# A hybrid decoder layer on one core: mask tiles in another pool, a reordered last head, two spare tiles in the output projection, later E loads, five buffers for the modulation sums

## The chip, the cores and the metric

The kernel runs on one core of a Trainium2 chip. TensorE (PE) multiplies matrices, VectorE (DVE) and ScalarE (ACT) do elementwise work, GpSimd (POOL) some masks, and SyncE (SP), ACT and POOL issue DMAs. Each engine takes its instructions in order, from a queue of its own, and waits on semaphores for the others. The metric is the device time of one execution in microseconds; the median of several runs counts.

## The reference

One layer, sequence 1024, width 1024, float32. The parts that matter here:

```python
mod = c_act @ w_ada + b_ada                # shifts, scales, gates: six vectors of 1024
u = x * (1.0 + sc1) + sh1
proj = u @ w_in                            # qa, ka, va, dq, dk, dv, z, b, a, g_a, g_b
y_a = sliding_window_attention(qa, ka, va, sinks) @ w_oa
# gated DeltaNet, 8 heads of 128, chunks of 64: decay matrices E, a triangular solve, a scan
o = gated_delta_rule(q, k, v, beta, g)
o = o * rsqrt(mean(o * o) + RMS_EPS) * norm_w * silu(z)
y_b = o @ w_ob
mixed = (sigmoid(g_a) * y_a + sigmoid(g_b) * y_b) @ w_out
x = layer_norm(ALPHA * x + (1.0 + gt1) * mixed)
# then the squared-ReLU MLP with 4096 hidden columns, and the second layer norm
```

## The kernel before

Every float32 product of the large projections is made of three: an operand is split into a high and a low part (`uh`, `ul` of the activations, `wh`, `wl` of the weights), and PE adds `uh*wh`, `ul*wh` and `uh*wl`. ACT copies the high part, DVE subtracts it from the raw tile to give the low one (for streamed weights the line with `wl<-wr,wh`). A *unit* (`stream_unit`) is one block of 128 output columns: two halves of 8 x 3 matmuls 128x512.

The program goes through these stages. First come the modulation, the value and key projections, and for each of the 8 DeltaNet heads the function `decays`: it makes `re` and `e` (the decay matrix E), `kd`, the products `kk` of a head's keys (`a<-kT`) and `mt`, and stores them in DRAM (`re_d`, `e_d`, `kd_d`, `md_d`, `l21_d`, which the trace calls `l_d`). In this stage the order of the engines comes from a scheduler; the tiles lie in the pool `pa`. From position `Q0` on the order is the program's own: `at(p, f)` puts the work of `f` at PE matmul number `p` (count[0]), `after(n, f)` at n later, and `vec`, `act`, `now` do so with a planner (`window`) that looks for room on DVE or ACT between the links of the scan. There `pa` is closed and the pool `pb` opens in its memory, with the tiles of the attention. The units of the remaining projections are PE's stream; the attention, the triangular solve (on DVE) and the scan over the heads are put between them.

In the scan head h starts at `R = R0 + 120 h` (PER = 120). `hd_load` fetches kT, E, Re, kd; `hd_kq` uses E (line 1189); `hd_a`, `hd_b`, `hd_c` make the chain over the eight chunks (`rhs`, `vn`, `o`, `St`); `hd_norm` with its `root` takes a square root on ACT, followed by a dummy SiLU that brings the SiLU table back; `hd_silu` is SiLU of z, `hd_out` multiplies and stores `og_d`. At the same time the modulation vectors that are needed later are summed up on DVE: `ada_load` fetches 128x512 of `w_ada` every 14 positions, `ada_add` adds it up (`ada<-adaw`). Units of kind `g_b` end in `gb_done`: copy on ACT (`gz`), store from ACT's queue.

At `OA` the output projection of the attention begins: products `(i, m)` of 12 matmuls each over operands `wo` and `q` (line 1558), in the order (0,1), (1,1), (0,6), (1,6), (0,7), (1,7), (0,4), (1,4), ... ; `q_part` splits the last pieces of the attention's result (`ts` into `qh`, `ql`, "11", "T2", "T3", "T4"). Each product is evicted by `o_part` (line 1510) into a tile of `o_tile`: tag `t0` in the pool `yo`, or `t` in the pool `p2`. `p2` exists only from position `CLOSE` on (`open_p2`), which closes the scan's pools and issues the first loads of further operands (`or`).

Of the kernel before, what the change touches and what calls it, by code (L numbers as in the profile page):

```python
# [9 lines left out]
F32 = mybir.dt.float32  # L10
F32R = mybir.dt.float32r
BF16 = mybir.dt.bfloat16
AF = mybir.ActivationFunctionType
ALU = mybir.AluOpType
# [3 lines left out]
P = 128  # L18
# [4 lines left out]
HALF = 512  # L23
# [4 lines left out]
NEG = -1e30  # L28
# [6 lines left out]
def hybrid_layer_kernel(ctx: ExitStack, tc: tile.TileContext,  # L35
                        x, c, w_ada, b_ada, w_in, conv_w, a_log, dt_bias, sinks, dn_norm_w,
                        w_oa, w_ob, w_out, ln1_g, ln1_b, w_ff1, b_ff1, w_ff2, b_ff2,
                        ln2_g, ln2_b, out, dbg=None):
    nc = tc.nc
    x, c, out = x[0], c[0], out[0]  # L40
# [6 lines left out]
    V, A, G, T = nc.vector, nc.scalar, nc.gpsimd, nc.tensor  # L47
# [9 lines left out]
    def brief(shape, name):  # L57
        return gpool.tile(shape, F32, name=name, bufs=1)
# [7 lines left out]
    def bc(ap, shape):  # L66
# [7 lines left out]
    gb_d = dram.tile([KT, P, S], F32, name="gb_d")  # L74
    og_d = dram.tile([KT, P, S], F32, name="og_d")
    kt_d = dram.tile([8, P, S], F32, name="kt_d")
    kd_d = dram.tile([8, P, S], F32, name="kd_d")
    e_d = dram.tile([8, P, S], F32, name="e_d")
# [17 lines left out]
    make_identity(nc, ident)  # L96
    ones = const.tile([P, P], F32, name="ones")
    V.memset(ones, 1.0)
    tri = brief([P, P], "tri")
    G.affine_select(out=tri, in_=ones, pattern=[[1, P]], compare_op=ALU.is_ge, fill=0.0,  # L100
                    base=0, channel_multiplier=-1)
    trim = brief([P, P], "trim")
    amask = brief([P, 2 * P], "amask")
    V.memset(amask, 0.0)
    G.affine_select(out=amask[:, 0:P], in_=amask[:, 0:P], pattern=[[1, P]], compare_op=ALU.is_gt,
                    fill=NEG, base=0, channel_multiplier=-1)
    G.affine_select(out=amask[:, P:2 * P], in_=amask[:, P:2 * P], pattern=[[-1, P]],
                    compare_op=ALU.is_ge, fill=NEG, base=0, channel_multiplier=1)
    eps_ln = const.tile([P, 1], F32, name="eps_ln")
    V.memset(eps_ln, LN_EPS)  # L110
    eps_rms = const.tile([P, 1], F32, name="eps_rms")
# [84 lines left out]
    halves = [slice(0, HALF), slice(HALF, 2 * HALF)]  # L196


    events, count, order = [], [0], [0]

    def at(p, f, *args):
        order[0] += 1
        heapq.heappush(events, (p, order[0], f, args))

    def after(n, f, *args):
        at(count[0] + n, f, *args)
# [86 lines left out]
    pv_pool = tc.tile_pool(name="pv", bufs=1, side="right")  # L293
    pv = pv_pool.__enter__()
    NV = 272
    wvh = pv.tile([P, KT, NV], F32R, name="wvh")
    wvl = pv.tile([P, KT, NV], F32R, name="wvl")
    p0_pool = tc.tile_pool(name="p0", bufs=1, side="right")
# [162 lines left out]
    for step in steps.split():  # L461
        f, k = step[0], int(step[1])
# [49 lines left out]
    with tc.tile_pool(name="pa", bufs=2, side="right") as pa:  # L512
        if True:
            ba = pv.tile([P, NT, 16], F32, name="ba")
            for t in range(NT):
                tok = slice(t * P, (t + 1) * P)
                pt = psum("ab"[t % 2], 2) if t < 4 else mm_tile()
# [29 lines left out]
            xs, y, r, z2, pl = (tmp(n) for n in ("xs", "y", "r", "z2", "pl"))  # L547
# [85 lines left out]
        for h in range(8):  # L633
# [41 lines left out]
            for b in range(2):  # L675
                r = slice(64 * b, 64 * b + 64)
# [15 lines left out]
    pb = pb_pool.__enter__()  # L692
    M = so.tile([P, 64, 64], F32, name="M")
    Mf = M.rearrange("p s c -> p (s c)")

    def solve_load():
        nc.scalar.dma_start(out=Mf, in_=md_d.rearrange("h b n s c -> (h b n) (s c)"))

# [258 lines left out]
    def big4(tag, dtype=F32, shape=None, bufs=2):  # L957
        return pc.tile(shape or [P, S], dtype, tag=tag, name=tag, bufs=bufs)

    HOP = 5  # L960
    PER = 3 * HOP * NT
    R0 = Q0 + 160
# [17 lines left out]
    def vec(lag, cost, f, *args):  # L980
        q = window("V", count[0] + lag, cost)
        at(q, f, *args)
        return q
# [64 lines left out]
    def ada_cols_of(f):  # L1048
        return (2, 5, 3, 4)[f // 2] * D + (f % 2) * HALF

    def ada_load(i, f, k):
        w, lo = ada["w"][i % 3], ada_cols_of(f)
        nc.sync.dma_start(out=w, in_=w_ada[k * P:(k + 1) * P, lo:lo + HALF])
        q = vec(36, 3.3, ada_add, w, k)
        if k == KT - 1:
            at(q + 7, ada_part, f)

# [42 lines left out]
    def hd_load(h):  # L1100
        d = heads[h]
        d["kT"], d["kd"], d["E"], d["Re"] = big4("kT"), big4("kd"), big4("E"), big4("Re", bufs=1)
        TT = d["TT"] = TTs[h % 2]
        T2o = d["T2o"] = big4("T2o", shape=[64, 4, 64], bufs=1)
        half = [slice(0, 64), slice(64, P)]
        nc.sync.dma_start(out=d["kT"], in_=kt_d[h])
        (nc.sync if h else nc.gpsimd).dma_start(out=d["E"], in_=e_d[h])
        nc.gpsimd.dma_start(out=T2o, in_=tt_d[h, 1, 1::2].rearrange("n s c -> s n c"))
        for i in range(2):
            nc.gpsimd.dma_start(out=TT[half[i], :, half[i]], in_=tt_d[h, i].rearrange("n s c -> s n c"))  # L1110
        nc.gpsimd.dma_start(out=d["Re"], in_=re_d[h])
        nc.gpsimd.dma_start(out=d["kd"], in_=kd_d[h])
        if h == 0:
            hd_solved(0)
        elif h < 7:
            hd_solved(h + 1)
        d["ssq"] = pc.tile([P, NT], F32, tag="ssq", name="ssq")
        d["sso"] = pc.tile([P, NT], F32, tag="sso", name="sso")
        d["vr"] = big4("vr")
        d["o"] = [big4(f"o{i}", shape=[P, HALF], bufs=2 - i) for i in range(2)]  # L1120
# [142 lines left out]
    def hd_norm(h):  # L1263
        d = heads[h]
        fs = pc.tile([P, NT], F32, tag="fs", name="fs")
        V.tensor_scalar(out=fs, in0=d["ssq"], scalar1=RMS_EPS * P * P, scalar2=None, op0=ALU.mult)
        V.tensor_tensor(out=fs, in0=fs, in1=d["sso"], op=ALU.add)

        def sc(n):
            if n % 2:  # L1270
                A.activation(out=o_chunk(d, n), in_=o_chunk(d, n), func=AF.Copy, scale=fs[:, n:n + 1])
            else:
                V.tensor_scalar(out=o_chunk(d, n), in0=o_chunk(d, n), scalar1=fs[:, n:n + 1], scalar2=None,
                                op0=ALU.mult)
        def root():
            A.activation(out=fs, in_=fs, func=AF.Sqrt, scale=1.0 / P, bias=eps_q)
            A.activation(out=d["sso"][:, 0:1], in_=d["ssq"][:, 0:1], func=AF.Silu)
            vec(9, 0.5, lambda: V.reciprocal(out=fs, in_=fs))
            vec(11, 5.5, lambda: [sc(n) for n in range(0, NT, 2)])
            act(11, 7, lambda: [sc(n) for n in range(1, NT, 2)] + [flags.add(("o", h))])  # L1280
        act(3, 13.5, root)

    def hd_out(h, half):
        d = heads[h]
        assert ("o", h) in flags
        tp = psum("b", 2)
        for j in range(4):
            T.transpose(tp[:, chunk(j)], o_chunk(d, 4 * half + j), ident)

        def put():  # L1290
            V.scalar_tensor_tensor(out=d["sz"][:, halves[half]], in0=tp, scalar=normw, in1=d["sz"][:, halves[half]],
                                   op0=ALU.mult, op1=ALU.mult)
            if half == 1:
                nc.gpsimd.dma_start(out=og_d[h], in_=d["sz"])
        now("V", 2, 3.3, put)

    def gb_done(i):
        ts = []

        def done(half, pt):  # L1300
            t = big4("gz", shape=[P, HALF])
            A.activation(out=t, in_=pt, func=AF.Copy)
            A.dma_start(out=gb_d[i, :, halves[half]], in_=t)
        return done

    for h in range(8):
        R = R0 + PER * h
        early = max(R - 118, OPEN + 1)
        at(early, hd_load, h)
        for half in range(2):  # L1310
            at(R - 45 + 15 * half, hd_kq, h, half)
            at(R - 40 + 15 * half, hd_qturn, h, half)
            at(R - 10 + 15 * half, hd_vturn, h, half)
            at(R + 122 + 8 * half, hd_silu, h, half)
        if h == 0:
            at(early + 50, hd_z, 0)
            at(early + 52, hd_solved, 1)
        at(R - 55 if h else R0 - 30, hd_x, h)
        at(R + 35, hd_gate, h)
        for n in range(NT):  # L1320
            at(R + 3 * HOP * n, hd_a, h, n)
            at(R + 3 * HOP * n + HOP, hd_b, h, n)
            at(R + 3 * HOP * n + 2 * HOP, hd_c, h, n)
        at(R + PER + 2, hd_norm, h)
        at(R + PER + (45 if h < 7 else 32), hd_out, h, 0)
        at(R + PER + (60 if h < 7 else 36), hd_out, h, 1)

    big2 = p2 = p2_pool = None
    L0 = Q0 + 48 * (len(units_h) - 1)
# [51 lines left out]
        split_s(*[t[:, k % 2, :] for t in quad[name, k // 2]], late[k][i][:, halves[u]], 5)  # L1381

    for name, ps_ in (("11", (-42, -39, -36, -33)), ("T2", (-29, -26, -23, -20)), ("T3", (-9, -6, 0, 4)),
                      ("T4", (8, 11, 16, 19))):
        for k in range(4):
            at(OA + ps_[k], q_part, name, k)

# [56 lines left out]
            stream_unit(uh, ul, gb_done(h), interleave=h == 7)  # L1444


    CLOSE = OA + 22
    oh, ol, ograw = [None] * KT, [None] * KT, {}

    def og_load(k):  # L1450
# [46 lines left out]
    ot = {}  # L1497

    def o_tile(i, c):
        if (i, c) in ((0, 0), (0, 2), (2, 0), (2, 2)):  # L1500
            ot[i, c] = yo.tile([P, HALF], F32, tag="t0", name="t0")
        else:
            ot[i, c] = p2.tile([P, HALF], F32, tag="t", name="t", bufs=5)
        return ot[i, c]
# [357 lines left out]
    def put(m, i, t, q=None):  # L1862
        (q or nc.sync).dma_start(out=hf_d[m - 1, i], in_=t)
# [428 lines left out]
```

## Time and profile before

| | |
|---|---|
| median of 3 runs | 1809.24 us (1808.39 to 1811.13) |
| the profiled execution | 1811.05 us, its span 1809.3 us |
| granted TensorE clock, mean | 0.995 |
| DVE, ACT, POOL busy | 72%, 58%, 18% |
| DMA, mean over the span | 194 GB/s |

The span runs from the first to the last instruction. A line of a timeline gives the start and the length of a group of instructions in us, the engine, the line in the kernel, the operation, output<-inputs with shapes, and in brackets the idle time just before it with what ended it. PE rows show the time until a result is out, about 0.39 us for a 128x512 matmul; as they are pipelined, the step from one to the next counts.

### The profile page before, as it was taken

The page shows a single profiled execution, that of the slowest core. Times are in us where ns is not written, and L with a number is a line of the kernel's source. Part 1 is how long each engine was busy: PE and PEld are TensorE (multiplying, and loading weights), DVE is VectorE, ACT ScalarE, POOL GpSimd, SP SyncE. Part 2 cuts the span into 40 slices and gives each one's busy share as a digit, 9 for nine tenths or more (in the row PEclk, how much of TensorE's full clock was granted, in tenths as well). Part 3 has the DMA queues.
Part 4 walks back from the last instruction along what each step waited for, and adds up shares of the span by engine and source line. Part 5 has one row for each costly group of instructions (what it writes and reads, how often), then busy time and mean ns, then how long its engine had stood idle before and what let it go on. Part 6 is the DMA issues. An engine that isn't in the chain of part 4 may idle for free.

```text
span 1809.3 us, 26356 instructions
## 1 busy us (share of the span) xinstructions
PE 1787.6 (99%) x9137; PEld 1504.0 (83%) x9137; DVE 1300.7 (72%) x2438; ACT 1046.4 (58%) x2371; POOL 318.8 (18%) x482
## 2 busy tenths in 40 slices
PE   8999999999999999999999999999999999999998
PEld 6988888888888888888878888878888888888887
DVE  6688688988856566767678455789777766676697
ACT  4699678888874556556475332475555554434341
POOL 0234234444331011110001210002222220000000
PEclk8999999999999999999999999999999999999999
DMA  9756722232256566655747644459887879755671
GB/s 280 207 201 204 229 71 90 62 110 74 85 195 199 137 178 177 171 182 176 245 141 249 215 151 143 147 163 333 284 287 272 287 275 391 250 187 186 204 262 47
DMA packets 268151, 350.32 MB, mean 194 GB/s; under 512 B 27009, under 2 KB 172114, under 8 KB 267762
## 3 DMA queue, kind: packets, MB, share of 16 engines
q1 hardware_dynamic: 225842, 220.27, 38.9%
q0 software_dynamic: 31728, 107.39, 17.7%
q10 hardware_dynamic: 10448, 20.98, 3.2%
q8 instruction: 72, 1.18, 0.3%
q14 instruction: 61, 0.50, 0.1%
HBM read 238.74 MB, written 107.75 MB: 191 GB/s over the span
## 4 chain that ended last, share of the span: by engine, by line
PE 89%; ACT 3%; DVE 2%; DMA 2%; issue 1%; POOL 0%; ACTq 0%; DVEq 0%; POOLq 0%
PE mm L262 34%; PE mm L2153 8%; PE mm L2213 7%; PE a L2213 4%; PE b L2153 4%; PE b L2213 4%; PE a L2153 3%; PE mm L1558 2%; PE mm L1782 2%; PE c L2213 2%; PE c L892 2%; PE a L1782 1%; PE b L1558 1%; PE mm L192 1%; PE mm L190 1%; PE mm L191 1%
## 5 line engine op out<-in xcount | busy, mean ns | idle before, releaser
L262 PE MATMUL mm<-uh,wh 128*128 128x512 f32 x800 | 319.8, 400 | 0.0
L262 PE MATMUL mm<-uh,wl 128*128 128x512 f32 x800 | 319.6, 399 | 0.0
L262 PE MATMUL mm<-ul,wh 128*128 128x512 f32 x800 | 318.8, 398 | 0.0
L220 DVE TENSOR_TENSOR sp<-sraw,sp 128x1024 fp32r<-128x1024 f32 x112 | 132.7, 1219 | 75.8 <-ACT sp L219 75.8
L219 ACT ACTIVATE sp<-sraw 128x1024 fp32r<-128x1024 f32 x112 | 112.6, 1053 | 121.4 <-PE b L2213 75.4
L262 PEld LDWEIGHTS mm<-uh,wh 128*128 128x128 f32 x800 | 150.7, 188 | 26.4
L262 PEld LDWEIGHTS mm<-ul,wh 128*128 128x128 f32 x800 | 150.8, 188 | 26.1
L262 PEld LDWEIGHTS mm<-uh,wl 128*128 128x128 f32 x800 | 150.8, 188 | 26.0
L2213 PE MATMUL mm<-sp 128*128 128x512 f32 x528 | 136.0, 389 | 0.0
L2213 PEld LDWEIGHTS mm<-sp 128*128 128x128 f32 x528 | 98.7, 188 | 20.5 <-DVE sp L220 0.2
L2213 PE MATMUL a<-sp 128*128 128x512 f32 x336 | 92.2, 389 | 0.0
L825 DVE CUSTOM_DVE_ANT_0 nscore<-a,amask,nsink 128x256 f32<-128x256 f32 (+1 forms) x128 | 54.5, 464 | 43.4 <-PE a L818 43.1
L1236 ACT ACTIVATE vn<-a,brk 128x128 f32<-128x128 f32 x64 | 23.6, 368 | 98.0 <-PE a L1234 95.9
L2213 PE MATMUL b<-sp 128*128 128x512 f32 (+1 forms) x336 | 79.6, 374 | 0.0
L2213 PEld LDWEIGHTS a<-sp 128*128 128x128 f32 x336 | 63.1, 188 | 13.1
L237 DVE TENSOR_TENSOR wl<-wr,wh 128x1024 fp32r<-128x1024 f32 x56 | 69.0, 1232 | 3.5 <-ACT wh L233 3.4
L836 POOL TENSOR_TENSOR sm<-sm 128x256 f32<-128x256 f32 x56 | 51.5, 920 | 103.6 <-ACT sm L832 72.8
L2213 PEld LDWEIGHTS b<-sp 128*128 128x128 f32 x336 | 60.3, 188 | 11.2
L220 DVE TENSOR_TENSOR wl<-fraw,wh 128x1024 fp32r<-128x1024 f32 x43 | 52.5, 1222 | 19.7 <-ACT wh L219 19.5
L832 ACT ACTIVATE sm<-nscore,stat 128x257 f32<-128x257 f32 (+1 forms) x128 | 62.0, 487 | 2.7 <-DVE stat L825 2.5
L219 ACT ACTIVATE wh<-fraw 128x1024 fp32r<-128x1024 f32 x43 | 45.0, 1055 | 31.0 <-PE b L2153 25.1
L877 POOL TENSOR_SCALAR_AFFINE_SELECT pl<-ph 128x512 fp32r<-128x512 f32 x56 | 53.7, 959 | 41.7 <-DVE ph L870 38.1
(563 smaller groups left out, 4757.6 us busy)
## 6 DMA issues: line engine op xcount, KB each, us to landing
wr<-in_w_in_dram SPq DMA_DIRECT2D x60, 512.0 KB, 3.8
sraw<-hf_d SPq DMA_DIRECT2D x54, 512.0 KB, 4.3
adaw<-in_w_ada_dram SPq DMA_DIRECT2D x74, 256.0 KB, 5.0
fraw<-in_w_ff_dram SPq DMA_DIRECT2D x32, 512.0 KB, 5.1
sraw<-wt_d SPq DMA_DIRECT2D x32, 512.0 KB, 4.3
hf_d<-t ACTq DMA_DIRECT2D x48, 256.0 KB, 4.5
wt_d<-wx POOLq DMA_DIRECT2D x48, 256.0 KB, 3.9
sraw<-in_w_ff_dram SPq DMA_DIRECT2D x22, 512.0 KB, 5.8
```

Of the source, the lines that this page charges most:

```text
L219: A.activation(out=hi, in_=src, func=AF.Copy)
L220: after(lag, lambda: V.tensor_tensor(out=lo, in0=src, in1=hi.bitcast(F32), op=ALU.subtract))
L237: V.tensor_tensor(out=hl[1], in0=raw, in1=hl[0].bitcast(F32), op=ALU.subtract)
L262: T.matmul(ts[half], lhsT=w[:, k, :], rhs=xx[k][:, sl], start=k == 0 and m == 0, stop=k == KT - 1 and m == 2)
L825: V.tensor_tensor_reduce(out=ns[:, i, 1:1 + W], in0=sc[:, i * 2 * P:i * 2 * P + W], in1=amask[:, mo:mo + W], scale=-1.0, scalar=nsink[:, 2 ...
L832: A.activation(out=sm[:, i, 0:1 + W], in_=ns[:, i, 0:1 + W], func=AF.Exp, scale=-1.0, bias=st[:, i:i + 1], accum_out=st[:, 2 + i:3 + i])
L836: G.tensor_tensor(out=sm[:, :, 1 + P:1 + 2 * P], in0=sm[:, :, 1:1 + P], in1=sm[:, :, 1 + P:1 + 2 * P], op=ALU.add)
L877: G.affine_select(out=flat4(part), in_=flat4(full), pattern=[[0, 4], [1 if odd else -1, P]], compare_op=ALU.is_ge if odd else ALU.is_gt, f ...
L1558: T.matmul(pt, lhsT=t[:, lw, k, :], rhs=r[:, k % 2, :], start=begin and k == 0 and x_ == 0, stop=k == 3 and x_ == 2, skip_group_check=True)
L1782: T.matmul(pt, lhsT=m[k][:, tok], rhs=w[:, k % 2, :], start=k == 0 and w is wh and m is mh, stop=k == KT - 1 and m is ml)
L2153: T.matmul(pt, lhsT=a[:, kk, :], rhs=b[k], start=begin and k == 0 and x_ == 0, stop=k == 3 and x_ == 2, skip_group_check=True)
L2213: T.matmul(to, lhsT=a[:, f, t * P:(t + 1) * P], rhs=b[:, f, lo:up], start=(begin or own) and s % NS == 0 and f == 0 and x_ == 0, stop=s % ...
```

## The change

It has six parts.

1. The masks `tri` and `trim` move from the start to the pool `pv`; `amask`, the mask of the attention, moves from the start of the program to the opening of `pb`.
2. The sums of the modulation get two more buffers (tiles with tag `t0`), five instead of three, and an add is due 42 instead of 36 positions after its load.
3. E of the heads 1 to 7 is loaded 40 positions later.
4. In the last head the SiLU of z stands 22 to 25 positions earlier, ahead of the root, and the dummy SiLU is left out; the output's halves come 3 positions earlier, and each is stored by itself on SP instead of one store on POOL.
5. `gb_done` places copy and store a little later where they would fall close ahead of `vn`.
6. The tiles of the products with c = 0 all use `t0`, with two buffers; `T4` is split 8 to 11 positions later and `p2` opens 10 positions later.

```diff
-    tri = brief([P, P], "tri")
-    ...
-    amask = brief([P, 2 * P], "amask")
-    V.memset(amask, 0.0)
     ...
+    tri = pv.tile([P, P], F32, name="tri")
     ...
     pb = pb_pool.__enter__()
     ...
+    amask = pb.tile([P, 2 * P], F32, name="amask", bufs=1)
+    V.memset(amask, 0.0)
+    G.affine_select(out=amask[:, 0:P], ...)
+    G.affine_select(out=amask[:, P:2 * P], ...)
     ...
     def ada_load(i, f, k):
-        w, lo = ada["w"][i % 3], ada_cols_of(f)
+        if i == 0:
+            ada["w"] += [yo.tile([P, HALF], F32, tag="t0", name="adaw", bufs=2) for _ in range(2)]
+        w, lo = ada["w"][i % 5], ada_cols_of(f)
         nc.sync.dma_start(out=w, in_=w_ada[k * P:(k + 1) * P, lo:lo + HALF])
-        q = vec(36, 3.3, ada_add, w, k)
+        q = vec(42, 3.3, ada_add, w, k)
     ...
-        (nc.sync if h else nc.gpsimd).dma_start(out=d["E"], in_=e_d[h])
+        if h:
+            after(40, lambda: nc.sync.dma_start(out=d["E"], in_=e_d[h]))
+        else:
+            nc.gpsimd.dma_start(out=d["E"], in_=e_d[h])
     ...
         def root():
             A.activation(out=fs, in_=fs, func=AF.Sqrt, scale=1.0 / P, bias=eps_q)
-            A.activation(out=d["sso"][:, 0:1], in_=d["ssq"][:, 0:1], func=AF.Silu)
+            if h < 7:
+                A.activation(out=d["sso"][:, 0:1], in_=d["ssq"][:, 0:1], func=AF.Silu)
     ...
-            if half == 1:
+            if h == 7:
+                nc.sync.dma_start(out=og_d[h, :, halves[half]], in_=d["sz"][:, halves[half]])
+            elif half == 1:
                 nc.gpsimd.dma_start(out=og_d[h], in_=d["sz"])
     ...
         def done(half, pt):
-            t = big4("gz", shape=[P, HALF])
-            ...
+            def put():
+                ...
+            p = count[0]
+            r = (p - R0) % 15
+            at(p + 7 - r if 2 < r < 7 else p, put)
     ...
-            at(R + 122 + 8 * half, hd_silu, h, half)
+            at(R + (122 + 8 * half if h < 7 else 100 + 5 * half), hd_silu, h, half)
     ...
-        at(R + PER + (45 if h < 7 else 32), hd_out, h, 0)
-        at(R + PER + (60 if h < 7 else 36), hd_out, h, 1)
+        at(R + PER + (45 if h < 7 else 29), hd_out, h, 0)
+        at(R + PER + (60 if h < 7 else 33), hd_out, h, 1)
     ...
-                      ("T4", (8, 11, 16, 19))):
+                      ("T4", (16, 19, 27, 30))):
     ...
-    CLOSE = OA + 22
+    CLOSE = OA + 32
     ...
     def o_tile(i, c):
-        if (i, c) in ((0, 0), (0, 2), (2, 0), (2, 2)):
-            ot[i, c] = yo.tile([P, HALF], F32, tag="t0", name="t0")
+        if c == 0:
+            ot[i, c] = yo.tile([P, HALF], F32, tag="t0", name="t0", bufs=2)
```

How it moves instructions shows at three places; all lines of the changed kernel up to the masks' new place have numbers lower by 6 to 10, those behind it higher by up to 13. The first is the end of `decays` on DVE. Before, at the beginning of head 6's second part (`rk` to `kd` belong to the head, `wl` is the low part of weights of a unit after `Q0`):

```order
L604 TENSOR_SCALAR e<-a,r 128x128 x4
L652 RECIPROCAL rk<-irk 128x8
L237 TENSOR_TENSOR wl<-wr,wh 128x1024
L653 TENSOR_TENSOR brk<-beta,rk 128x8
L656 TENSOR_TENSOR kdc<-ekd,rk 128x8
L654 SCALAR_TENSOR_TENSOR nbrk_684<-brk,rk 128x8
```

After, the end of the same stage, head 7 (`kll` and `qs` are the attention's keys and queries):

```order
L648 SCALAR_TENSOR_TENSOR nbrk_676<-brk,rk 128x8
L654 TENSOR_TENSOR kd<-b,kdc 128x512
L654 TENSOR_TENSOR kd<-c,kdc 128x512
L666 SCALAR_TENSOR_TENSOR mt<-a,nbrk_676,e 128x128 x8
L691 MEMSET amask 128x256
L227 TENSOR_TENSOR wl<-wr,wh 128x1024 x2
L767 TENSOR_TENSOR kll<-ks,khh 64x512 x3
L227 TENSOR_TENSOR wl<-wr,wh 128x1024
L767 TENSOR_TENSOR kll<-ks,khh 64x512
L787 SCALAR_TENSOR_TENSOR qs<-mm,qs 64x512 x4
```

The memset of `amask` now stands behind the last `mt` of head 7, and the `wl` of the first two units, one of which stood between `rk` and `brk` of head 6 (the other one head earlier), stand behind the memset.

The second place is PE there. Before, from the first matmul of the first unit (`uh_127` and `ul_135` are block 0 of the activations, `a<-kT` the `kk` of head 7):

```order
L262 MATMUL mm<-uh_127,wh 128x512
L262 MATMUL mm<-ul_135,wh 128x512
L262 MATMUL mm<-uh_127,wl 128x512
L262 MATMUL mm<-uh_128,wh 128x512
L262 MATMUL mm<-ul_136,wh 128x512
L669 MATMUL a<-kT 128x128 x4
L262 MATMUL mm<-uh_128,wl 128x512
L262 MATMUL mm<-uh_129,wh 128x512
L262 MATMUL mm<-ul_137,wh 128x512
L262 MATMUL mm<-uh_129,wl 128x512
L262 MATMUL mm<-uh_130,wh 128x512
L669 MATMUL a<-kT 128x128 x4
```

After (block 0 is `uh_116` and `ul_124`):

```order
L252 MATMUL mm<-uh_123,wl 128x512
L252 MATMUL mm<-uh_116,wh 128x512
L252 MATMUL mm<-ul_124,wh 128x512
L663 MATMUL a<-kT 128x128 x4
L252 MATMUL mm<-uh_116,wl 128x512
L252 MATMUL mm<-uh_117,wh 128x512
L252 MATMUL mm<-ul_125,wh 128x512
L252 MATMUL mm<-uh_117,wl 128x512
```

The first matmul on `wl` stood ahead of both `kk` groups; now it stands behind them, as the unit's third matmul.

The third place is ACT at the beginning of the output projection, before:

```order
L1302 ACTIVATE gz<-mm 128x512
L1303 DMA gb_d<-gz 128x512
L219 ACTIVATE wo<-owg 128x512
L219 ACTIVATE qh<-ts 128x512 x2
L219 ACTIVATE wo<-owr 128x512
L219 ACTIVATE qh<-ts 128x512
L1510 ACTIVATE t_10286<-mm 128x512
L219 ACTIVATE qh<-ts 128x512
L219 ACTIVATE wo<-owg 128x512
L219 ACTIVATE wo<-owr 128x512
L219 ACTIVATE qh<-ts 128x512
L1510 ACTIVATE t<-mm 128x512
```

After:

```order
L1312 ACTIVATE gz<-mm 128x512
L1313 DMA gb_d<-gz 128x512
L1312 ACTIVATE gz<-mm 128x512
L1313 DMA gb_d<-gz 128x512
L209 ACTIVATE wo<-owr 128x512
L1523 ACTIVATE t_10283<-mm 128x512
L209 ACTIVATE qh<-ts 128x512
L209 ACTIVATE wo<-owg 128x512
L209 ACTIVATE wo<-owr 128x512
L209 ACTIVATE qh<-ts 128x512
L1523 ACTIVATE t_10310<-mm 128x512
```

`t` are the evictions of the first two products, `qh` on `ts` the split pieces, `wo` on `owr` and `owg` the operands. Between the root and the first `t` stood nine splits `qh`, three `wo`, one SiLU of z and a second table load (`L1277 ACT_TABLE_LOAD`); now seven `qh` and three `wo`, without SiLU and table load.

More of the change, by code (lines that the diff above doesn't have):

```diff
@@ L98, in hybrid_layer_kernel @@
     V.memset(ones, 1.0)
-    tri = brief([P, P], "tri")
-    G.affine_select(out=tri, in_=ones, pattern=[[1, P]], compare_op=ALU.is_ge, fill=0.0,
-                    base=0, channel_multiplier=-1)
-    trim = brief([P, P], "trim")
-    amask = brief([P, 2 * P], "amask")
-    V.memset(amask, 0.0)
[L105 to L108, printed above, removed]
     eps_ln = const.tile([P, 1], F32, name="eps_ln")
@@ L295, in hybrid_layer_kernel @@
     NV = 272
+    tri = pv.tile([P, P], F32, name="tri")
+    G.affine_select(out=tri, in_=ones, pattern=[[1, P]], compare_op=ALU.is_ge, fill=0.0,
+                    base=0, channel_multiplier=-1)
+    trim = pv.tile([P, P], F32, name="trim")
     wvh = pv.tile([P, KT, NV], F32R, name="wvh")
@@ L694, in hybrid_layer_kernel @@
     Mf = M.rearrange("p s c -> p (s c)")
+    amask = pb.tile([P, 2 * P], F32, name="amask", bufs=1)
+    V.memset(amask, 0.0)
+    G.affine_select(out=amask[:, 0:P], in_=amask[:, 0:P], pattern=[[1, P]], compare_op=ALU.is_gt,
+                    fill=NEG, base=0, channel_multiplier=-1)
+    G.affine_select(out=amask[:, P:2 * P], in_=amask[:, P:2 * P], pattern=[[-1, P]],
+                    compare_op=ALU.is_ge, fill=NEG, base=0, channel_multiplier=1)
     def solve_load():
@@ L1300, in done @@
         def done(half, pt):
-            t = big4("gz", shape=[P, HALF])
-            A.activation(out=t, in_=pt, func=AF.Copy)
-            A.dma_start(out=gb_d[i, :, halves[half]], in_=t)
+            def put():
+                t = big4("gz", shape=[P, HALF])
+                A.activation(out=t, in_=pt, func=AF.Copy)
+                A.dma_start(out=gb_d[i, :, halves[half]], in_=t)
+            p = count[0]
+            r = (p - R0) % 15
+            at(p + 7 - r if 2 < r < 7 else p, put)
         return done
```

## The prediction

> **What bounds the kernel now.** I read the page first: the engines' busy time, the slices with the granted TensorE clock, and the chain that ended last.
>
> ```profile
> span 1809.3 us, 26356 instructions
> ## 1 busy us (share of the span) xinstructions
> PE 1787.6 (99%) x9137; PEld 1504.0 (83%) x9137; DVE 1300.7 (72%) x2438; ACT 1046.4 (58%) x2371; POOL 318.8 (18%) x482
> ...
> PE 89%; ACT 3%; DVE 2%; DMA 2%; issue 1%; POOL 0%; ACTq 0%; DVEq 0%; POOLq 0%
> ```
>
> PE is busy 99% of the span and is 89% of the chain, so the time moves only by what makes PE stand still, or by its clock. Next I took the table of what PE waited for (total, times, longest), since every row of it is a gain that the change could have.
>
> ```profile
> PE mm L1558 <- ACT t L1510: 2.9, 2, 1.5
> ...
> PE c L1257 <- DVE o L1261: 0.9, 1, 0.9
> ...
> PE b L1288 <- DVE o L1273: 0.7, 1, 0.7
> PE a L1245 <- ACT vn L1236: 0.6, 1, 0.6
> ```
>
> The first row is the output projection, the next three are the scan over the heads. All four together are 5.1 us, 0.3% of the time: that is nearly all this change can win. From three runs within 0.15%, no change means about 0.2%, or 3.6 us. What is left to find is what it can lose, and that needs the places where instructions now stand elsewhere.
>
> **The masks.** `amask` now lives in the pool `pb`, which opens on the memory of the closed pool `pa`. Its memset therefore waits for the last readers of `pa`: head 7's `mt`, and the stores of `kd`, `md`, `l` (SP) and `re`, `e` (POOL) out of it. As one reader is a store, the wait ends only when it has landed. Behind that memset in DVE's queue stand the two `wl` subtractions for the first two units of the next stage; before, they stood in heads 5 and 6 of `decays`. The timelines of DVE, SP, ACT and PE at that place (start, length, what):
>
> ```profile
> 202.38 2.16 DVE L672 SCALAR_TENSOR_TENSOR mt<-a,nbrk,e 128x128 f32<-128x128 f32 x8 [1.27 <-POOL e L608]
> 209.85 2.00 DVE L766 TENSOR_TENSOR kll<-ks,khh 64x512 fp32r<-64x512 f32 x3 [5.31 <-ACT khh L761]
> 212.11 1.23 DVE L237 TENSOR_TENSOR wl<-wr,wh 128x1024 fp32r<-128x1024 f32 x1 [0.26 <-ACT wh L233]
> ...
> 205.99 0.65 SPq L678 DMA_DIRECT2D l_d<-mt  x1
> ...
> 209.19 0.63 ACT L761 ACTIVATE khh<-ks 64x512 fp32r<-64x512 f32 x1 [8.00 <-DMA l_d<-mt]
> ...
> 201.16 1.05 PE L669 MATMUL a<-kT 128*128 128x128 f32 x8
> 201.97 0.48 PE L262 MATMUL mm<-ul,wh 128*128 128x512 f32 x1
> ...
> 221.26 0.11 DVE L700 MEMSET M<- 128x64 f32 x1
> ...
> 202.21 17.69 PE mm L262 x78
> ```
>
> The row at 209.19 shows the mechanism in the old kernel: `khh`, also a tile of `pb`, held ACT 8.00 us until `l_d` had landed. It cost nothing, as PE needed none of it. The new memset is the same wait, but on DVE, with work behind it that PE needs.
>
> When would PE get there? The last row gives the dense step, 17.69 / 78 = 0.227 us. At 201.97 the old PE had done both `kk` groups of head 7 and ten matmuls of the first unit; in the new order the third matmul of that unit (the first on `wl`) comes after both groups and two, so PE is there at 201.97 - 8 x 0.227 = 200.15. When is `wl` ready? In the old kernel the stores had landed by 209.19. Two `wl` of 1.23 have left DVE ahead of head 7's chain, but that chain also runs through ACT and POOL (`mt` waited 1.27 for POOL), so I take 1.0 us earlier, between 0 and 2.46. The memset is 128x256; 128x64 took 0.11, so between 0.11 and 0.44, I take 0.25 as nearer to a fixed part plus four times the work. Then 208.2 + 0.25 + 1.23 = 209.7, and PE stands from 200.15 to 209.7: +9.5 us (8.0 to 10.7). Nothing covers it: the instruction behind it on PE is the same unit, in order. ACT and DVE run late by no more than PE does, so nothing is late next. Of the rest of this part, `tri` in another pool and POOL's two selects (POOL is busy 18%) cost nothing: the scores that use the masks come behind the same stall.
>
> The Trainium skill, DMA: Bandwidth & Descriptors, Anatomy of one DMA, puts a DMA's fixed cost at some 2 us, mostly the receipt of the last byte. By it the 64 KB store issued at 205.99 would be in at about 208.0 and the stall 1.2 us shorter, by an estimate from that figure; the 3.2 us from issue to `khh` in the row decide.
>
> **The clock after such a pause.** The windows of 1 us around the start (PE busy is the second number, PEclk the first after the engines):
>
> ```profile
> 31.00:32.00 1.00, 0.06 (x1) 0.00 (x0) 0.65 (x2) 0.00 (x0) 0.00 (x0) 1.00 1.14 310
> 32.00:33.00 1.00, 0.41 (x3) 0.33 (x3) 0.96 (x5) 0.59 (x1) 0.00 (x0) 1.00 0.91 256
> 33.00:34.00 1.00, 1.00 (x5) 0.84 (x6) 0.82 (x3) 1.00 (x3) 0.00 (x0) 0.84 1.03 292
> 34.00:35.00 1.00, 1.00 (x4) 0.81 (x3) 0.98 (x2) 1.00 (x2) 0.00 (x0) 0.50 1.06 289
> ...
> 37.00:38.00 1.00, 1.00 (x12) 1.00 (x10) 0.22 (x1) 0.00 (x0) 0.00 (x0) 0.95 1.14 317
> ...
> 931.00:935.00 4.00, 2.72 (x12) 2.17 (x12) 4.00 (x8) 3.32 (x7) 0.00 (x0) 1.00 0.33 133
> ```
>
> After 1.5 us without work (31 to 33) the clock was 0.50 from about 33.7 to 37.1: 0.32 us of the first slice, three whole ones, 0.1 of the last, 3.4 us. In the projection 1.3 us of idle time in four did not lower it. A pause of 9.5 us is six times the one that did, so I count on it. The price is half of the slow time: 3.4 / 2 = +1.7 us; between 0.8 (half that) and 3.4 (twice).
>
> The Trainium skill, TensorE: Matmul & The Clock Gate, Part 1, says that an idle window of about 3.4 us halves the clock and that about as long of steady work restores it. The trace agrees on 3.4 us for the slow stretch; by the page it would be the same 1.7.
>
> **The projection.** Timelines of ACT, PE, DVE and SP:
>
> ```profile
> 918.65 1.28 ACT L1276 ACT_TABLE_LOAD   x1
> ...
> 920.25 1.28 ACT L1277 ACT_TABLE_LOAD   x1
> 921.55 0.20 ACT L1277 ACTIVATE sso<-ssq 128x1 f32<-128x1 f32 x1
> ...
> 931.65 0.57 ACT L1510 ACTIVATE t<-mm 128x512 f32<-128x512 f32 x1
> ...
> 936.08 0.60 ACT L1510 ACTIVATE t<-mm 128x512 f32<-128x512 f32 x1 [1.77 <-PE mm L1558]
> ...
> 930.37 0.39 PE L1558 MATMUL mm<-qh,wo 128*128 128x512 f32 x1
> 932.28 0.50 PE L1558 MATMUL mm<-qh,wo 128*128 128x512 f32 x1 [1.52 <-ACT t L1510]
> ...
> 935.32 0.68 DVE L220 TENSOR_TENSOR ql<-ts,qh 128x512 fp32r<-128x512 f32 x1
> ...
> 936.38 0.88 SPq L1372 DMA_DIRECT2D or<-attn_d  x2
> ```
>
> From 930.37 to 932.28 are 1.91 us where 0.23 was due: the first eviction `t` started at 931.65, behind a full ACT queue. The second waited for the pool `p2`, which opens after the last split of `T4` (935.32 + 0.68 = 936.0): the page blames PE, but 936.08 is that end. Both stalls are 2.9 us of waiting and some 0.3 of restarting. Now the table reload and dummy (1.28 + 0.20) are gone for this head, its SiLU of `z` (0.62 twice) comes before the stage, and the two first tiles need no pool. So ahead of the first `t` ACT has 1.5 us of table and dummy less, one SiLU (0.6) and two splits (0.6 each): 3.3 us, of which some 0.4 turn into waiting for products. It comes at 928.8, and PE needs it at 930.6; the second, two `wo` and two `qh` later, at 931.7, needed 12 matmuls on, at 933.3. The pool opens with `T4`'s last split, walked to 934.6, 1.4 earlier than before although it was moved later in the program, since PE is not held. Late next: the first two `qh` on `or` (2.00 for both) now stand ahead of the fourth `t`, about 0.3. So 3.2 - 0.3 = -2.9 us (-3.3 to -1.6). The store of the last head by halves on SP stands among the issues of loads there; the program reads it back over 100 matmuls later, which hides it; without that cover it would cost a store's landing, 3.2 us by the row of `l_d`.
>
> **Scan: sums, E, gates.** DVE's waits, the issue of E and its users:
>
> ```profile
> DVE ada L1063 <- DMA adaw<-in_w_ada_dram: 5.8, 4, 2.2
> ...
> 618.20 8.52 SPq L1107 DMA_DIRECT2D E<-e_d  x1
> ...
> 709.16 1.94 SPq L1107 DMA_DIRECT2D E<-e_d  x1
> ...
> 691.01 1.13 DVE L1189 SCALAR_TENSOR_TENSOR E<-b,rk,E 128x128 f32<-128x128 f32 x4 [0.54 <-PE b L1185]
> 733.63 1.12 DVE L1189 SCALAR_TENSOR_TENSOR E<-b,rk,E 128x128 f32<-128x128 f32 x4 [0.54 <-PE b L1185]
> ...
> DMA to landing us min/median/max: 7.1/8.3/9.7
> ...
> 904.60 0.60 ACT L1302 ACTIVATE gz<-mm 128x512 f32<-128x512 f32 x1 [1.65 <-PE mm L262]
> 905.60 0.37 ACT L1236 ACTIVATE vn<-a,brk 128x128 f32<-128x128 f32 x1 [0.41 <-ACT gz L1302]
> ```
>
> DVE's four waits for modulation weights (longest 2.2 us) are where both `o` rows of PE's table come from: `o` stands behind them. An add is now due 6 positions later; from head to head, 120 positions, E's first use moves from 691.0 to 733.6, so a position is 0.355 us and the six are 2.1 us. That alone nearly covers 2.2, and E's issue, which blocked SP for 8.52 us, leaves the burst. Gain 0.9 + 0.7 = -1.6 us (-2.1 to 0, if the burst only shifts). E itself comes 40 positions, 14.2 us, later. At its shortest it was issued 24.5 us before its first use (709.16 to 733.63), so 10.3 us are left against landings of 7.1 to 9.7: nothing, by a hair. `gz` moves behind `vn` at 905, worth about 0.1 (0 to 0.9); the 0.6 at `vn` stays, as two table loads, `vr` and `gz` still stand ahead of it there.
>
> **Sum.** +9.5 + 1.7 - 2.9 - 1.6 - 0.1 = +6.6 us. The profiled span is 1809.3 (its run 1811.05), the median of the runs 1809.24, so 1815.8. With the ends of the terms: +1.8 to +12.5, or 1811 to 1821.7.
>
> **Rivals.**
> - The memset is not held by the stores (its memory was free, or DVE reaches it late anyway). For it: I read the overlap from the order, and no trace shows this memset. Against: the 8.00 us of `khh`. Both first terms go: -4.6, 1804.6. It decides when the stall is under 1 us, that is when `wl` is ready by 201.
> - Half of it: head 7's chain and its stores end 4 or 5 us earlier and the pause is too short to touch the clock: 4.7 - 4.6, about 1809.4.
> - The change doesn't do what it says in the projection: the wait goes to the fourth `t` behind the `or` splits. Against: 2.00 us is about their whole cost. Gain lost: 1818.7.
> - E comes late: under load a landing over 10.3 us stalls DVE, with PE behind, in up to seven heads, 0.7 each: +5, 1820.8.
>
> **How the numbers follow.** Forecast 0.58 (own range 1811 to 1820.5), memset free 0.10, half 0.12, projection's wait moved 0.12, E late 0.08. Leaving out the first rival and most of E late gives 1808 to 1820.5. Faster by over 0.2%: 0.10; within: 0.13, the half case and an edge of mine; slower: 0.77.
>
> **What would show it.** After: PE waiting 8 to 10 us for `wl` near 200, after a DVE memset that waits for `l_d`, then some 3.4 us at clock 0.50; no wait of PE for `t` in the projection over 0.5; no DVE wait for `adaw` over 0.5; no wait for E. I am wrong if PE goes on at 200, or if the scan shows new DVE waits on DMAs.

## The result, and the profile after

The changed kernel takes 1821.56 us (median of 4 runs, 1819.64 to 1822.75) against 1809.04 for the kernel before (4 runs, 1808.39 to 1811.13): ratio 1.0065, 95% interval [1.0052, 1.0079]. It is slower, as forecast, but by 12.5 us and not by 6.6; 1821.56 is just above the end of the range, 1820.5.

The head of the page after, and the table of what PE waited for (total, times, longest):

```profile
span 1821.0 us, 26363 instructions
PE 1792.1 (98%) x9137; PEld 1508.7 (83%) x9137; DVE 1299.6 (71%) x2438; ACT 1044.3 (57%) x2369; POOL 320.1 (18%) x481
...
PE mm L252 <- DVE wl L227: 8.9, 1, 8.9
PE mm L1571 <- ACT t L1523: 3.1, 1, 3.1
...
PE a L1251 <- ACT vn L1242: 0.6, 1, 0.6
```

The number of matmuls is the same, and yet PE is busy 4.5 us longer (1792.1 for 1787.6): a part of its work ran slower. The two `o` rows are gone from the table; the two waits for `t` in the projection are one, longer than both; and the wait for `wl` is new.

The place of the masks, on DVE and PE:

```profile
201.42 2.16 DVE L666 SCALAR_TENSOR_TENSOR mt<-a,nbrk,e 128x128 f32<-128x128 f32 x8 [1.95 <-POOL e L602]
207.96 0.27 DVE L691 MEMSET amask<- 128x256 f32 x1 [4.39 <-DMA l_d<-mt]
208.15 2.38 DVE L227 TENSOR_TENSOR wl<-wr,wh 128x1024 fp32r<-128x1024 f32 x2
...
209.37 0.80 PE L252 MATMUL mm<-uh,wl 128*128 128x512 f32 x1 [8.94 <-DVE wl L227]
209.96 0.63 PE L252 MATMUL mm<-uh,wh 128*128 128x512 f32 x1
210.38 0.63 PE L252 MATMUL mm<-ul,wh 128*128 128x512 f32 x1
```

The memset waits for `l_d`, the two `wl` come behind it, and PE behind the first of them. After the pause the step of the same matmul is 0.42 us and not 0.227. The windows (length, busy times, then PEclk) show why, here and again in the projection:

```profile
204.00:208.00 4.00, 0.00 (x0) 0.00 (x0) 0.04 (x1) 0.24 (x1) 0.00 (x0) 0.67 0.57 140
208.00:209.00 1.00, 0.00 (x0) 0.00 (x0) 1.00 (x2) 0.97 (x3) 0.64 (x1) 0.50 1.07 180
209.00:212.00 3.00, 2.63 (x6) 2.17 (x7) 2.97 (x5) 0.57 (x1) 3.00 (x5) 0.50 0.69 262
212.00:215.00 3.00, 3.00 (x8) 2.35 (x8) 0.54 (x1) 0.00 (x0) 1.77 (x4) 0.50 1.07 373
215.00:216.00 1.00, 1.00 (x4) 0.76 (x3) 0.00 (x0) 0.00 (x0) 0.00 (x0) 0.70 0.68 159
...
954.00:956.00 2.00, 2.00 (x6) 1.54 (x5) 1.79 (x3) 1.38 (x3) 0.00 (x0) 0.50 0.91 269
...
958.00:960.00 2.00, 2.00 (x7) 1.57 (x6) 1.45 (x2) 1.17 (x2) 0.00 (x0) 0.58 1.02 349
```

PE resumes at 209.37 and runs at half clock until about 215.6. In the projection the same lasts from 953.48 to 959.7. That second place on ACT, SP and PE:

```profile
950.55 1.06 ACT L209 ACTIVATE qh<-or 128x1024 fp32r<-128x1024 f32 x1 [4.49 <-DMA or<-attn_d]
951.89 1.06 ACT L209 ACTIVATE qh<-or 128x1024 fp32r<-128x1024 f32 x1 [0.28 <-DMA or<-attn_d]
952.85 0.58 ACT L1523 ACTIVATE t<-mm 128x512 f32<-128x512 f32 x1
...
942.92 0.38 SPq L1407 DMA_DIRECT2D owr<-in_w_oa_dram  x1
944.11 0.89 SPq L1385 DMA_DIRECT2D or<-attn_d  x2
...
953.48 0.80 PE L1571 MATMUL mm<-qh,wo 128*128 128x512 f32 x1 [3.14 <-ACT t L1523]
```

ACT stood idle for 4.49 us, waiting for the `or` load of the split `qh`; behind that split and the next stood the eviction `t` of product (0,7), the fifth one, whose result had long been there. PE needed this eviction to go on with (0,4) in the same bank.

Two matmuls mark the stages in both traces: the scan's first one on `St`, and the projection's first one. Before and after:

```profile
582.00 0.38 PE L1224 MATMUL a<-St,kT 128*128 128x128 f32 x2
924.56 0.48 PE L1558 MATMUL mm<-qh,wo 128*128 128x512 f32 x1
...
593.85 0.38 PE L1230 MATMUL a<-St,kT 128*128 128x128 f32 x2
933.39 0.39 PE L1571 MATMUL mm<-qh,wo 128*128 128x512 f32 x1
```

The books of the profiled runs, 1821.0 - 1809.3 = +11.7 us, follow from them: +11.85 up to the scan (593.85 for 582.00), -3.02 in the scan (339.54 for 342.56), and +2.87 from the projection to the end. At 158.7 us the run after was only 0.2 behind, so the first stage is that of the masks; the slow stretch at 33.7 to 37.1, which the run after hasn't, makes no difference that lasts.

The pieces are these. The pause for `wl`, from one matmul's start to the next 9.2 instead of 0.2, is +9.0; half clock after it, 14 matmuls of 0.44 instead of 0.227, +3.0. In the projection the old pauses are -3.3, the new one +3.3, half clock after it +3.0. In the scan PE's idle time fell from 2.5 to 0.6 us; where the other 1.1 comes from was not told apart.

### The profile page after: what moved, and what is told of

Its sections match the earlier page's. It is cut to its first block, busy times and chain, and to the rows that moved or that the text cites. A ratio compares the mean times of both kernels' runs of the same rounds, so it can differ in the third digit from the quotient of the medians.

```text
span 1821.0 us, 26363 instructions
## 1 busy us (share of the span) xinstructions
PE 1792.1 (98%) x9137; PEld 1508.7 (83%) x9137; DVE 1299.6 (71%) x2438; ACT 1044.3 (57%) x2369; POOL 320.1 (18%) x481
## 4 chain that ended last, share of the span: by engine, by line
PE 88%; ACT 4%; DVE 3%; DMA 1%; issue 1%; POOL 0%; ACTq 0%; SPq 0%; DVEq 0%; POOLq 0%
PE mm L252 34%; PE mm L2166 8%; PE mm L2226 7%; PE a L2226 4%; PE b L2166 4%; PE b L2226 4%; PE a L2166 3%; PE mm L1795 2%; PE c L2226 2%; PE mm L1571 2%; PE c L893 2%; PE a L1795 1%; PE b L1571 1%; PE mm L182 1%; PE mm L180 1%; PE mm L181 1%
## 5 line engine op out<-in xcount | busy, mean ns | idle before, releaser
L2226 PEld LDWEIGHTS b<-sp 128*128 128x128 f32 x336 | 60.4, 188 | 11.2
L223 ACT ACTIVATE wh<-wr 128x1024 fp32r<-128x1024 f32 x56 | 59.0, 1053 | 12.8 <-DMA wr<-in_w_in_dram 12.7
```

The source lines that it names most:

```text
L223: A.activation(out=hl[0], in_=raw, func=AF.Copy)
L2226: T.matmul(to, lhsT=a[:, f, t * P:(t + 1) * P], rhs=b[:, f, lo:up], start=(begin or own) and s % NS == 0 and f == 0 and x_ == 0, stop=s % ...
```

## The experiments

All ratios are to runs of the kernel before on the same chip, whose median there was 1810.2 to 1810.5 us. The experiments were made on two chips, so they are compared with each other and with the changed kernel by these ratios; 0.001 is 1.8 us.

**1. Part 1 alone.** The kernel before, with the masks moved as in the change and nothing else.

```diff
 (kernel before)
-    amask = brief([P, 2 * P], "amask")
     ...
+    amask = pb.tile([P, 2 * P], F32, name="amask", bufs=1)   # where pb opens
+    V.memset(amask, 0.0)
     ...
```

> The kernel before with part 1 of the change alone (masks in other pools, amask set at the opening of pb). Theory A (mask on DVE): the whole of the stall near 200 us comes with this part: PE waits 8.5 to 10 us for wl, then the clock is at half for 3.4 to 7 us, in all +11 to +13 us, about 1821. The projection's two waits for t (1.5 and 1.4 us) and the scan's waits stay as before. Rival B (the stall comes from the scheduler's other order of decays, moved by other parts): no wait over 1 us there, 1809.

1821.75 us, ratio 1.0063 [1.0046, 1.0080]. PE's waits:

```profile
PE mm L252 <- DVE wl L227: 8.9, 1, 8.9
...
PE mm L1559 <- ACT t L1511: 3.0, 2, 1.5
```

Part 1 alone costs 11.6 us, as theory A said; the projection is as before. The other five parts together thus came out near zero on top of it. The scan's waits did not stay as before, against A: of the two `o` rows 0.2 is left, though the scan's code is the old one, so these waits change from run to run.

**2. The mask on another engine.** The changed kernel, with one letter different.

```diff
-    V.memset(amask, 0.0)
+    G.memset(amask, 0.0)
```

> The changed kernel with one word other: the memset of amask is issued on GpSimd instead of VectorE. The mask still waits for the stores out of the closed pool, but on a queue that PE does not need. Theory A: PE's wait of 8.9 us and the slow clock behind it go together, 9.0 + 3.0 = 12 us less than the changed kernel, about 1809.5; the wait of 3.1 us for t in the projection with its slow clock stays. Rival B (the slow clock has another cause than the pause): 9 us less and a stretch of clock 0.50 near 210 us stays, about 1812.5. Rival C (the wait only moves, to the keys of the attention or to its first scores): PE waits 5 us or more near 220 us, about 1815.

1810.67 us, ratio 0.9998 [0.9989, 1.0008]: some 12 us less than the changed kernel. On GpSimd:

```profile
209.46 0.31 POOL L691 MEMSET amask<- 128x256 f32 x1 [6.19 <-DMA l_d<-mt]
```

The memset waits for the same store as before, 6.19 us, and nothing that PE needs at once stands behind it. PE's wait for `wl` and the slow clock at 210 are gone together (A; B falls). C holds in small at most: PE stands 0.7 us ahead of the attention's first scores, at 220, but as much stands there in a run with the old masks too (experiment 4).

The ten times fall into two groups: three at 1807.7, seven at 1810.2 to 1812.2, the former with a mean clock of 0.995 to 0.996, the latter of 0.993 to 0.994. In the profiled run, one of the three, the projection's wait for `t` was 2.7 us and the clock stayed up:

```profile
938.00:942.00 4.00, 1.26 (x6) 0.76 (x5) 1.95 (x2) 2.87 (x4) 0.00 (x0) 1.00 0.92 309
942.00:945.00 3.00, 3.00 (x14) 2.42 (x14) 2.33 (x3) 1.73 (x4) 0.00 (x0) 1.00 0.80 239
```

So a pause near 3 us need not drop the clock: it did in the changed kernel (3.14 us) and did not here. A drop in the seven slower runs would explain the 3 us between the groups and their lower mean clock; it is not shown, as none of the seven was profiled.

**3. Evictions ahead of the late splits.** On top of 2, the first four splits of `or` behind the evictions of (0,7) and (1,7).

```diff
-    RSPLIT = (54, 60, 66, 86, 104, 112)
+    RSPLIT = (74, 75, 80, 88, 104, 112)
```

> As mask_pool, and the first four splits of the operands that the projection loads late (or into qh, ql) stand at positions 74, 75, 80, 88 instead of 54, 60, 66, 86, so behind the evictions t of products (0,7) and (1,7) in ACT's queue. Theory A (t stood behind splits that wait for their DMA): no wait of PE for t over 0.5 us, no slow clock in the projection, 3.3 + 3.0 = 6.3 us less than mask_pool, about 1803.5; at most 1 us of it comes back as a wait for the first products on or. Rival B (t is late for lack of ACT time, or the loads themselves are what PE needs): the wait moves to the first product on or, 2 us or more there, within 2 us of mask_pool.

1806.44 us, ratio 0.9979 [0.9970, 0.9989]: 4.2 us less than experiment 2, on the same chip. ACT and PE's waits:

```profile
936.63 0.60 ACT L1523 ACTIVATE t<-mm 128x512 f32<-128x512 f32 x1 [1.60 <-PE mm L1571]
939.35 0.60 ACT L1523 ACTIVATE t<-mm 128x512 f32<-128x512 f32 x1 [2.12 <-PE mm L1571]
939.84 2.06 ACT L209 ACTIVATE qh<-or 128x1024 fp32r<-128x1024 f32 x2
...
PE b L1571 <- DVE t L1349: 1.3, 1, 1.3
```

Both evictions now wait for PE and for nothing else, and no wait of PE for them is left. A part comes back: 1.3 us at a later product, whose bank DVE is late to free, probably since the splits reach it later. The gain is less than A gave (1803.5 plus at most 1). The clock stays up there in the profiled run, and the ten times no longer fall into two groups (1804.7 to 1808.2).

**4. Four pauses made on purpose.** In the dense stretch of the b projection of the kernel before, PE waits for a chain of ACT copies.

```diff
 (kernel before)
+    def pause(n):
+        s = amask[:, 0:P]
+        t = psum("b", 2)
+        T.matmul(t[:, 0:P], lhsT=ident, rhs=ident, start=True, stop=True)
+        A.activation(out=s, in_=t[:, 0:P], func=AF.Copy)
+        for _ in range(n):
+            A.activation(out=s, in_=s, func=AF.Copy)
+        T.matmul(t[:, P:2 * P], lhsT=s, rhs=ident, start=True, stop=True)
+
+    for n, p in ((2, 50), (5, 130), (9, 210), (24, 290)):
+        at(count[0] + p, pause, n)
```

> The kernel before with four made pauses in the dense stretch of the b projection (1005 to 1092 us before): PE multiplies a 128x128 identity, ACT copies the result 1 + n times one after the other (n = 2, 5, 9, 24), PE multiplies by the copy and goes on. By the copies' 0.26 to 0.37 us each PE should stand about 1.3, 2.2, 3.4 and 8 us. Theory A (the clock goes by idle time, and the phase of a fixed window decides): nothing after the first, clock 0.50 for 3 to 7 us after the last and the one before, the second between; each slow stretch costs half of its length, in all about 15 us of pauses and 4 to 10 us of slow clock. Rival B (the slow clock near 210 us has nothing to do with idle time): clock 1.00 after all four, 15 us in all.

1833.17 us, 23 more than before: some 16 us of pauses and 4.6 of slow clock, both by the steps between the matmuls, and the added matmuls with their restarts. The four pauses in PE's timeline, and windows behind them:

```profile
1017.11 0.49 PE L1589 MATMUL b<-ident,amask 128*128 128x128 f32 x2 [1.05 <-ACT amask L1588]
...
1038.04 0.49 PE L1589 MATMUL b<-ident,amask 128*128 128x128 f32 x2 [2.07 <-ACT amask L1588]
...
1062.01 0.49 PE L1589 MATMUL b<-ident,amask 128*128 128x128 f32 x2 [3.44 <-ACT amask L1588]
...
1091.06 0.80 PE L1589 MATMUL b<-ident,amask 128*128 128x128 f32 x2 [8.55 <-ACT amask L1588]
...
1018.00:1022.00 4.00, 4.00 (x20) 3.30 (x19) 0.72 (x2) 1.47 (x3) 1.07 (x2) 1.00 0.75 217
1038.00:1042.00 4.00, 3.96 (x13) 3.19 (x14) 0.00 (x0) 1.89 (x2) 0.00 (x0) 0.68 0.35 104
1042.00:1045.00 3.00, 3.00 (x12) 2.40 (x12) 1.58 (x3) 0.17 (x1) 0.00 (x0) 0.86 0.00 0
1062.00:1066.00 4.00, 4.00 (x13) 3.28 (x14) 1.69 (x3) 1.17 (x2) 0.01 (x1) 0.66 0.00 0
1082.00:1091.00 9.00, 0.51 (x4) 0.27 (x2) 2.45 (x4) 7.69 (x26) 0.00 (x0) 0.79 0.05 18
1091.00:1095.00 4.00, 3.94 (x12) 3.29 (x13) 0.69 (x1) 2.42 (x4) 0.53 (x1) 0.62 0.05 11
```

Idle time does it: after 1.05 us nothing; after 2.07 a stretch of (1 - 0.68) x 4 x 2 + (1 - 0.86) x 3 x 2 = 3.4 us at half clock; after 3.44 about as much; with 8.55 twice that, 0.21 x 9 x 2 + 0.38 x 4 x 2 = 6.8 us, of which 3.8 fell into the pause itself and cost nothing. B falls.

The slow stretch need not start with PE's return: after 2.07 us PE ran at full clock for 1.3 us first. By the rows the three stretches begin at 1039.4, 1063.3 and 1087.2. That is 23.9 us apart both times, 7 x 3.41, though the pauses ended 1.4 us before, 1.3 us before and 3.9 us after these points. So in this run the clock changes on a grid of 3.41 us that the pauses do not move. In the changed kernel's mask pause it was three pieces of this length (0.33 x 4 x 2 = 2.6 up to 208, 7 to 215, 0.6 to 216: 10.2), of which 6.2 fell on PE's work.

The Trainium skill, TensorE: Matmul & The Clock Gate, Part 1, has the clock go by a window of 3413 ns that runs freely. The pieces of 3.4 and the grid agree. The idle window of about 3.4 us that the prediction cites from the same part is longer than what was needed here, 2.07 us.

**5. Part 6's positions back.** On top of 2: T4's splits and the opening of `p2` where they were before; the two tiles stay.

```diff
-                      ("T4", (16, 19, 27, 30))):
+                      ("T4", (8, 11, 16, 19))):
     ...
-    CLOSE = OA + 32
+    CLOSE = OA + 22
```

> As mask_pool (mask set by GpSimd), with T4's splits and CLOSE of part 6 back at their old positions (8, 11, 16, 19 and OA+22); the two t0 tiles stay. Theory A (the fourth t waits for the or loads, whose landing follows the opening of p2): the pool opens and the or loads are issued 1 to 2 us earlier against PE, and ahead of the owr load, so PE's wait of 2.7 to 3.1 us for t falls to 0.5 to 1.5 us and the clock no longer drops there; the first two t, with two more qh ahead of them, come 1 us later and still in time. 3 to 5 us less than mask_pool's slow-clock runs, about 1806.5. Rival B (part 6 is right and the positions are needed for the first t): a wait of 1 us or more returns for the first or second t, no gain.

1805.86 us, ratio 0.9976 [0.9965, 0.9987], by the ratios 4 us less than experiment 2. SP, ACT, and where the projection starts on PE:

```profile
923.63 0.40 PE L1571 MATMUL mm<-qh,wo 128*128 128x512 f32 x1
...
936.56 1.06 ACT L209 ACTIVATE qh<-or 128x1024 fp32r<-128x1024 f32 x1 [0.24 <-DMA or<-attn_d]
938.88 0.58 ACT L1523 ACTIVATE t<-mm 128x512 f32<-128x512 f32 x1
...
932.61 0.89 SPq L1385 DMA_DIRECT2D or<-attn_d  x2
...
934.05 0.47 SPq L1407 DMA_DIRECT2D owr<-in_w_oa_dram  x1
```

The `or` loads are issued 9.0 us after the projection's first matmul, against 10.7 in the changed kernel (933.39 to 944.11), and the first split can start 3.9 us after the issue instead of 6.4: here `owr` stands behind them in SP's queue, there it stood ahead. The edit moves the issue and the order together; but the other two profiled runs in which the splits stood idle for these loads had `owr` ahead too, and took 6.1 us (experiment 2) and 5.6 (experiment 7). ACT no longer waits over 0.3 us for the loads ahead of this eviction, and PE does not wait for any `t` of the projection. Theory A, with more than it promised; the first two evictions were in time without the later splits, so B falls.

**6. Both edits.** Experiments 3 and 5 together.

> Both edits on mask_pool: T4 and CLOSE at the old positions, and the or splits behind the evictions (74, 75, 80, 88). Theory A: neither t waits, and the or operands land earlier, so that the wait of 1.3 us for DVE's t of mask_pool_rsplit (DVE is full then) shrinks too: 1804.5 to 1806, the best of all here. Rival B (DVE's work of that stage sets the 1.3 us, whenever the loads land): as mask_pool_rsplit, 1806.4.

1806.36 us, ratio 0.9977 [0.9968, 0.9986], no different from either. Of the wait of 1.3 us, 0.7 is left:

```profile
PE b L1571 <- DVE t L1349: 0.7, 1, 0.7
```

The loads land early now, so this part probably comes of the splits' late places on DVE; A is half right. With part 6's positions back, moving the splits is of no use.

**7. Part 6 without parts 2 to 5.** The kernel before, the masks moved but set by GpSimd, and the two tiles with the later positions.

> The kernel before with the masks moved, but set by GpSimd (the two tiles don't fit otherwise), and part 6 alone: two t0 tiles, later T4 and CLOSE. Parts 2 to 5 are left out. Theory A (part 6 turns the two waits for the first t's into one for the fourth): no PE wait for the first two t over 0.6, one of 2 to 3.5 us for t behind qh on or; clock 0.50 after it in some runs. 1808 to 1812, no gain over the kernel before. Rival B (the new wait comes of the last head's part 4, whose stores on SP stand ahead of the or loads): no wait over 1 us, about 1806.5.

1813.47 us, ratio 1.0018 [1.0009, 1.0027].

```profile
PE mm L1559 <- ACT t L1511: 4.4, 3, 3.0
```

The three waits are for the first, the third and the fifth `t` (0.5, 0.9 and 3.0 us). A's long wait is there, behind `qh` on `or` as A said, but at the fifth `t` and not the fourth; the clock fell to 0.50 for 3.4 us after it. The first `t` keeps 0.5 without the shorter root and the earlier SiLU of part 4. The third, which needs the pool `p2`, keeps 0.9. From the projection's first matmul to the end this run takes 3.7 us more than the kernel before, so part 6 loses there by itself, and the new wait does not come of part 4. The median holds other things too: a wait of 1.6 us ahead of the scan, for the solve's `T`, which the kernel before has not, stands in this run.

**8. Parts 2 and 3 undone** on top of experiment 3: three buffers, 36 positions, E early.

> As mask_pool_rsplit, with parts 2 and 3 undone: three buffers, adds due after 36 positions, E loaded early. Theory A (those parts take the DVE waits for modulation weights away, and PE gets 0.3 to 2.3 us of it, by the run): four or five DVE waits for adaw of 1 to 2.2 us return, PE waits for o or rhs of 0.1 to 0.9 us return, 0.5 to 2 us more than mask_pool_rsplit. Rival B (my forecast: always 1.6 us): PE's waits at the o rows sum up to 1.6 us or more.

1807.70 us, ratio 0.9985 [0.9976, 0.9994], against 0.9979 [0.9970, 0.9989] with those parts: about 1 us, and the intervals overlap. DVE's waits for modulation weights come back, and one of PE's:

```profile
DVE ada L1064 <- DMA adaw<-in_w_ada_dram: 3.8, 3, 1.6
...
PE c L1258 <- DVE o L1262: 0.3, 1, 0.3
```

In the changed kernel DVE has no such wait. So the parts do what they say, on DVE. What PE gets of it changes with the run: from the scan's first matmul on `St` to the projection's first, the five profiled runs with these parts take 339.3 to 339.6 us, the five without them 339.8 to 342.6, and the profiled run of the kernel before is the longest of these.

## Why the prediction was right and wrong

- **The masks: right, mechanism and size.** Forecast +9.5; measured 9.0. `mt` came 0.96 us earlier (201.42 for 202.38), the memset took 0.27, `wl` was ready at 209.4. Experiments 1 and 2 show that it is the memset's place in DVE's queue, not the wait as such.
- **The clock: right mechanism, too small.** Forecast +1.7, with an end at 3.4; measured 3.0. The step that failed is "The price is half of the slow time: 3.4 / 2": one stretch of 3.4 us was taken over from the pause at the start, but a pause of 9 us held three, and 6.2 us of them came after PE's return.
- **The projection: wrong, and the largest miss.** Forecast -2.9; measured 0.0 for the waits (3.3 for 3.3) and +3.0 of clock. The failed step is "Late next: the first two `qh` on `or` (2.00 for both) now stand ahead of the fourth `t`, about 0.3". It priced the time of these splits on ACT, and took the operands as landed. They were issued 10.7 us after the start, as walked within a microsecond, but ACT could split the first only 6.4 us later; the load of `owr` had gone out ahead of them. (They stood ahead of the fifth `t`, as they did in the kernel before, where they had landed in time.) That was the third rival's place, "the wait goes to the fourth `t` behind the `or` splits", argued against with the same 2.00. And a pause of 3.1 us is long enough for the clock, a price that the prediction charged to the masks only. With part 6's old positions (experiment 5) the time from the projection's start to the end is 3.4 us shorter than in the kernel before, near the 2.9 of the forecast: with the rest of the change in place, the later positions lost it.
- **The first two evictions: right.** `t` at 936.90 and 939.69 is 3.5 and 6.3 us after the projection's start (933.39), against 4.2 and 7.1 in the forecast; neither holds PE.
- **The scan: right on DVE, not safe on PE.** The forecast of -1.6 took both `o` waits from one execution. The same scan code showed 0.2 us of it in experiment 1. In this pair of profiles the scan gave 3.0.
- **E: in time, but not for the reason given.** The prediction let E come "40 positions, 14.2 us, later", with 10.3 us left for a landing. The landings that the trace after shows took 7.5 to 13.3 us, and DVE still did not wait. E was issued as early as before: 24.2 us ahead of its use at the closest, where the kernel before had 24.5. So the outcome was luck; why the 40 positions do not show as time is open. The closest pair on SP and DVE:

```profile
761.01 0.66 SPq L1111 DMA_DIRECT2D E<-e_d  x1
785.23 1.12 DVE L1195 SCALAR_TENSOR_TENSOR E<-b,rk,E 128x128 f32<-128x128 f32 x4 [0.54 <-PE b L1191]
```

- **`gz`: right.** The 0.6 at `vn` stays, and the small stall at 906 (0.07 us) is gone.
- **The sum.** From 6.6 it goes by +0.65 (masks and clock, 11.85 for 11.2), -1.32 (scan and `gz`, 3.02 for 1.7) and +5.77 (projection to the end, +2.87 for -2.9) to 11.7, the difference of the profiled runs; the medians differ by 12.5. The low ends of the prediction's terms add up to +2.5, not to the +1.8 that it states.

The version with the lowest ratio is that of experiment 5: the change, with the memset on GpSimd and part 6's positions back, beats the kernel before by 0.24% [0.13%, 0.35%] and the changed kernel by about 0.9%. Experiments 3 and 6 lie within its interval.

## What to carry to other kernels

A tile that opens in the memory of a closed pool waits for that pool's last stores, and so does everything behind its first writer in that engine's queue: let an idle engine write it first. An instruction that waits for a load must not stand ahead of an eviction that waits for nothing; price the load's landing, with what is queued ahead of it, and not the instruction. And where TensorE is the bound, a pause of 2 us or more can cost more than itself, here up to 3.0 us more.

## What the runs showed of the hardware

The clock fell for one to three pieces of 3.4 us after idle times of 2.07, 2.95, 3.14, 3.44, 8.55 and 8.94 us, and not after 1.05, nor after the kernel before's 1.5 and 1.4 in the projection, nor after 2.74 us in experiment 2's profile. The grid fits this. The 2.07 us lay almost whole in one piece, from 1036.0 to 1039.4. The 2.74 us (939.05 to 941.79) were cut by an edge of that run's grid: its slow stretch at the start ends at 22.54, and 269 pieces of 3.413 later is 940.7, so 1.7 us lay before the edge and 1.1 behind it. So 2 us of idle time in one piece were enough, and 1.7 were not. The drop at 33.7 in the kernel before, with 1.5 us of idle time among very small matmuls, does not fit and stays open.

A pause's extra price, by the matmuls' steps, was 1.4 to 3.0 us, and the length of the pause does not order it: 2.07 and 3.44 us cost 1.6 each, 8.55 cost 1.4, 3.14 and 8.94 cost 3.0. With 8.55 us PE came back 0.45 us behind an edge (1090.6), and that piece was the last slow one; with 3.14 and 8.94 it came back 0.6 us behind one (952.9, 208.8), and one more slow piece followed.
